# A hybrid decoder layer on one core: recurrence scores in 32-token blocks on quarters of TensorE's array, a query tile in another PSUM bank, and softmax, compression and start-up steps in another order

## The chip, the cores and the metric

The kernel runs on one core of a Trainium2 chip. The metric is the device time of one execution in microseconds (us). A core has five engines that run their own instruction streams side by side: TensorE (PE; its weight loads are listed as PEld), VectorE (DVE), ScalarE (ACT), GpSimd (POOL) and SyncE (SP), which only starts transfers. They meet at semaphores. TensorE multiplies a stationary operand (the weights, up to 128 x 128, loaded first) by a moving one and writes to PSUM, eight banks of 128 partitions x 512 fp32 values. Its 128 x 128 array can be split by columns into two groups of 64 or four of 32, each with weights and an output of its own.

## The reference

One layer on x of shape (1, 1024, 1024), fp32: a feed-forward half step, a token mixer, a second feed-forward half step and a last norm. The mixer's width is shared by an attention of 8 heads of 64 in two key groups (three branches: compressed, selected and window, each with its own softmax and a gate) and a gated linear recurrence of 4 heads of 128.

```python
h = h + 0.5 * swiglu(rms_norm(h, ffn1_norm), ffn1_w_gu, ffn1_w_down)
h = h + hybrid_mixer(rms_norm(h, mix_norm), ...)
h = h + 0.5 * swiglu(rms_norm(h, ffn2_norm), ffn2_w_gu, ffn2_w_down)
return rms_norm(h, final_norm)
# mixer: parts = split(h @ w_in); concat(o_nsa, o_hg) @ w_out

# compressed keys and values of the attention
flat = blocks.transpose(0, 1, 3, 2, 4).reshape(B, nb, G, CMP_LEN * dk)
kc = gelu(flat @ w1) @ w2
# attention, for each of the three branches
p = softmax(where(valid, q @ k.T * scale - slope * dist, NEG)); o = p @ v
o = g[..., 0:1] * o_cmp + g[..., 1:2] * o_sel + g[..., 2:3] * o_win

# recurrence, chunk by chunk of 64 tokens
b = jnp.cumsum(lf, axis=2)                        # lf = log of the forget gate
decay = jnp.exp(where(tril, b[:, :, :, None, :] - b[:, :, None, :, :], NEG))
a = jnp.einsum('bhtd,bhtsd,bhsd->bhts', qc, decay, kc)
o = a @ vc + (qc * jnp.exp(b)) @ state
state = jnp.exp(b_last) * state + (kc * jnp.exp(b_last - b)).T @ vc
```

The decayed scores `a` can be had as plain products: two tokens that fall into different halves of a block of 2m tokens have their decay split at the middle of the block, one factor on the query, one on the key.

## The kernel before

**Dense work.** Every fp32 product of the layer's large matrices is three fast matmuls of 128 x 128 x 512 (high and low parts of both operands, `mm3`, L162 to L164; the same with 256 columns at L769 to L771 and for the down projections at L704 to L706). The splits into parts are made by GpSimd or ScalarE (high, L154 and L156) and VectorE (low, L158). Other work is laid between these matmuls: generators yield after a small piece, and the loops in `body` step them in turn. The order in which the code emits instructions is the order on each engine.

**Scores of the recurrence** (`hgrn_unit`, from L853). A unit is one head and one half of the sequence, 512 tokens in four groups `c` of 128; the two halves of a head are stepped together, so there are four pairs of units. Keys `k` and queries `q` lie as 128 channels x 512 tokens. For the base and for each of seven levels (block size 2m, m = 1 to 64), `score` multiplies keys by queries into a PSUM bank of tag "b", VectorE scales the second half of each block of q and the first half of each block of k by the decay (L893, L894), and the scores of that level are copied under a mask into `B` (L897). Base and levels 0 to 5 compute eight products of 64 x 64 (two per group of 128 tokens, on column groups 0 and 64 of the array, `mm64`); level 6, the off-diagonal 64 x 64 block of each 128, four. Each step yields, and the dense projection that the loop at L1520 walks through runs between two steps. `A` holds the finished score matrix of 128 x 128 per group.

**Compression** (`compress`, L1025 and L1048) is the first thing that this loop steps (hh = 0), with the projection of head 0 as the dense work; its weight tiles `w1` are loaded by ScalarE's queue into four buffers as they come free. What is left of the dense work runs after the steps.

**Query tiles** (`att_proj_q`). Each of four tiles of a half is a bank of 128 x 512; after its 24 dense matmuls ScalarE copies (L1100) and VectorE subtracts (L1101), twice, and the bank is free. At L1544 tiles 0 and 1 of the first half both use tag "b". The next stage's projection starts in tag "b" as well.

**Softmax** (`att_soft`). For each key group and block of 128 queries, four heads hh = 0 to 3 are taken one after the other. Scores of the three branches are reduced by VectorE (L1191), `rest()` takes the exponential on ScalarE with its row sums (L1228); after every second head VectorE inverts the sums of both heads in one instruction (L1232) and GpSimd scales the rows of both, three instructions a head (L1238). `att_pv` then transposes the scaled rows of all four heads on TensorE (L1269).

**Start and the norm chain.** At the start eight slices of x are split (L399, L400), and from kt = 5 the first products' copies out of PSUM (`pp`, L576) stand between them. In the first down projection, a table `after` hooks steps of the next norm (`first`, `cols`) behind certain tiles.

Of the kernel before, what the change touches and what calls it, by code (L numbers as in the profile page):

```python
# [9 lines left out]
F32 = mybir.dt.float32  # L10
F32R = mybir.dt.float32r
I32 = mybir.dt.int32
U8 = mybir.dt.uint8
# [58 lines left out]
class Net:  # L72
# [709 lines left out]
    def mixer_consts(self, tp):  # L782
# [11 lines left out]

        self.id64 = c.tile([128, 64], F32, name="id64")
        for o in (0, 64):
            r, k = slice(o, o + 64), slice(o, o + 64)
            nc.vector.tensor_copy(out=self.id64[r], in_=self.ident[r, k])
            nc.vector.tensor_copy(out=up[r, 64:], in_=xf[r, k])
        xf, up = up[:, 64:], up[:, :64]  # L800
        self.lev = []
        for l in range(5):
            m = 1 << l
            nc.vector.tensor_scalar(up, xf, float(m), None, op0=OP.is_ge)
            k = c.tile([128, 64], U8, name=f"lev{l}")
            nc.vector.scalar_tensor_tensor(out=k[:], in0=xf, scalar=float(2 * m), in1=up,
                                           op0=OP.is_lt, op1=OP.mult)
            self.lev.append(k)
# [45 lines left out]
    def hgrn_unit(self, p, t, half, states, mo):  # L854
# [8 lines left out]

        def mm64(out, part, a, b):
            mm(out[part * 64:part * 64 + 64], k[:, a:a + 64], q[:, b:b + 64], start=True, stop=True,  # L865
               tile_position=(0, part * 64), skip_group_check=True)

        def score(last=False):
            b = self.bank("b")
            for c in range(4):  # L870
                o = c * 128
                if last:
                    mm64(b[:, c // 2 * 64:c // 2 * 64 + 64], c % 2, o, o + 64)
                else:
# [8 lines left out]
        nc.vector.tensor_tensor(out=B[:], in0=b, in1=self.id64[:, None, :].to_broadcast([128, 4, 64]), op=OP.mult)  # L883
        yield
        F, o = f[:], 0
        for l in range(7):
            m = 1 << l
            n = 512 // (2 * m)
            b = score(l == 6)
            F2 = F.rearrange("p (n two) -> p n two", two=2)  # L890
            qv = q[:].rearrange("p (n two m) -> p n two m", two=2, m=m)[:, :, 1, :]
            kv = k[:].rearrange("p (n two m) -> p n two m", two=2, m=m)[:, :, 0, :]
            nc.vector.tensor_tensor(out=qv, in0=qv, in1=F2[:, :, 0:1].to_broadcast([128, n, m]), op=OP.mult)  # L893
            nc.vector.tensor_tensor(out=kv, in0=kv, in1=F2[:, :, 1:2].to_broadcast([128, n, m]), op=OP.mult)  # L894
            nc.vector.tensor_tensor(out=ft[:, o:o + n], in0=F2[:, :, 0], in1=F2[:, :, 1], op=OP.mult)
            if l < 5:
                nc.vector.copy_predicated(out=B[:], mask=self.lev[l][:, None, :].to_broadcast([128, 4, 64]), data=b)  # L897
            elif l == 5:
                for i in (0, 64):
                    nc.scalar.activation(out=B[i:i + 32, :, 32:64], in_=b[i:i + 32, :, 32:64], func=AF.Copy)  # L900
                for i in (0, 64):
                    nc.scalar.activation(out=A[i:i + 64, :, i:i + 64], in_=B[i:i + 64], func=AF.Copy)
            else:
                for i in range(2):
                    nc.scalar.activation(out=A[0:64, i::2, 64:128], in_=b[i * 64:i * 64 + 64, 0:2, :], func=AF.Copy)
            F = ft[:, o:o + n]
            o += n
            yield
# [252 lines left out]
    def att_soft(self, p, g, qb, hh):  # L1161
# [147 lines left out]
def body(ctx, tc, ins, out):  # L1309
# [37 lines left out]
    with cs:  # L1347
# [138 lines left out]

    after[6, 2] = first
    for m, n in zip(range(6, 11), (1, 2, 1, 2, 2)):
# [10 lines left out]
    if True:  # L1499
# [9 lines left out]
        with cw:  # L1509
            with ExitStack() as ch:  # L1510
# [257 lines left out]
```

## Time and profile before

| | us |
|---|---|
| three runs | 2004.4, 2007.15, 2007.25 (median 2007.15) |
| the profiled execution | 2007.51 |
| its span (first to last instruction) | 2005.8 |
| TensorE busy | 1976.2 (99%) |
| VectorE busy | 1390.7 (69%) |
| ScalarE busy | 793.1 (40%) |
| GpSimd busy | 501.7 (25%) |

The span is what the hardware profiler recorded between the first and the last instruction; 1.7 us of the execution lie outside it. Busy time counts an engine's own instructions, and for TensorE the ends of its pipelined matmuls are modelled. The chain that ended last is found by going back from the last instruction, at each step to what released it. The granted clock is 1.00 for TensorE at 2.4 GHz and 0.50 at 1.2 GHz; over the whole execution its mean is 0.997.

### The profile page before, as it was taken

To read this page: it belongs to the slowest core of one execution; us is meant where nothing else is said; L and a number is where in the kernel's file an instruction comes from. 1 tells how busy PE (TensorE), PEld (TensorE's weight loads), DVE (VectorE), ACT (ScalarE), POOL (GpSimd) and SP (SyncE) were. 2 spreads that over 40 slices of the span, in tenths; PEclk is the share of its full clock that TensorE was granted. 3 is DMA by queue.
4 is the path that set the end of the run, shared out by engine and by line. 5 is a ranking of instruction groups with operands and counts; after the bars stand their busy time and mean duration, and the time that the engine had idled before them with its cause. 6 is when DMAs were issued, how large, how long until landed. Compare 5 with 4: busy or idle time off the path is not lost.

```text
span 2005.8 us, 30977 instructions
## 1 busy us (share of the span) xinstructions
PE 1976.2 (99%) x10862; PEld 1661.2 (83%) x10862; DVE 1390.7 (69%) x2843; ACT 793.1 (40%) x1673; POOL 501.7 (25%) x594
## 2 busy tenths in 40 slices
PE   9999999999999999999999999999999999999998
PEld 6888888888888889889877788898888888888886
DVE  5987778658766546766358887746766677558677
ACT  5533333322233323332368776645333333323233
POOL 2133233234331000100035534301112222123221
PEclk9999999999999999999999999999999999999999
DMA  5345666348662233332211022452446566157564
GB/s 190 118 133 196 216 213 227 105 161 282 221 226 103 98 106 116 138 119 106 90 64 38 17 67 77 148 210 95 148 169 213 200 218 212 59 178 254 195 206 139
DMA packets 157116, 304.30 MB, mean 152 GB/s; under 512 B 17536, under 2 KB 39072, under 8 KB 156960
## 3 DMA queue, kind: packets, MB, share of 16 engines
q1 hardware_dynamic: 146896, 285.78, 41.9%
q10 hardware_dynamic: 10064, 16.53, 2.3%
q8 instruction: 86, 1.41, 0.3%
q14 instruction: 70, 0.57, 0.1%
HBM read 213.65 MB, written 88.60 MB: 151 GB/s over the span
## 4 chain that ended last, share of the span: by engine, by line
PE 93%; DVE 3%; ACT 1%; POOL 1%; issue 1%; DMA 1%; SPq 0%; DVEq 0%; ACTq 0%; POOLq 0%
PE b L162 17%; PE b L163 16%; PE b L164 16%; PE b L706 7%; PE b L704 7%; PE b L705 7%; PE b L769 3%; PE b L771 3%; PE b L770 3%; PE b L1269 3%; PE b L1260 3%; PE b L865 2%; PE b L1185 1%; PE b L1186 1%; POOL P L1238 1%
## 5 line engine op out<-in xcount | busy, mean ns | idle before, releaser
L163 PE MATMUL b<-xT,wp 128*128 128x512 f32 x1196 | 466.8, 390 | 1.1 <-DVE xT L400 1.0
L162 PE MATMUL b<-xT,wp 128*128 128x512 f32 x1196 | 466.9, 391 | 0.7 <-ACT xT L399 0.7
L164 PE MATMUL b<-xT,wp 128*128 128x512 f32 x1196 | 465.9, 390 | 0.0
L158 DVE TENSOR_TENSOR dw<-dr,dw 128x512 fp32r<-128x512 f32 x308 | 234.5, 809 | 74.3 <-ACT dw L156 61.5
L162 PEld LDWEIGHTS b<-xT,wp 128*128 128x128 f32 x1196 | 224.9, 188 | 50.1 <-issue 2.0
L163 PEld LDWEIGHTS b<-xT,wp 128*128 128x128 f32 x1196 | 224.9, 188 | 48.8 <-DVE xT L400 2.7
L164 PEld LDWEIGHTS b<-xT,wp 128*128 128x128 f32 x1196 | 224.9, 188 | 46.9
L704 PE MATMUL b<-dw,dw 128*128 128x512 f32 x616 | 240.5, 390 | 1.1 <-DVE dw L158 1.1
L706 PE MATMUL b<-dw,dw 128*128 128x512 f32 x616 | 240.1, 390 | 0.2 <-DVE dw L158 0.2
L705 PE MATMUL b<-dw,dw 128*128 128x512 f32 x616 | 240.0, 390 | 0.0
L156 ACT ACTIVATE wp<-ws 128x512 fp32r<-128x512 f32 x148 | 93.3, 632 | 252.8 <-PE b L163 239.0
L154 POOL TENSOR_SCALAR dw<-dr 128x512 fp32r<-128x512 f32 x154 | 123.2, 806 | 275.0 <-PE b L706 158.6
L156 ACT ACTIVATE dw<-dr 128x512 fp32r<-128x512 f32 x154 | 92.4, 628 | 205.7 <-PE b L704 98.0
L1238 POOL TENSOR_SCALAR P<-P,sm,gate 128x64 f32<-128x64 f32 (+8 forms) x192 | 125.1, 669 | 176.3 <-DVE sm L1232 120.5
L158 DVE TENSOR_TENSOR wp<-ws,wp 128x512 fp32r<-128x512 f32 x148 | 111.3, 754 | 40.4 <-ACT wp L156 40.2
L704 PEld LDWEIGHTS b<-dw,dw 128*128 128x128 f32 x616 | 115.7, 188 | 25.5 <-issue 1.8
L706 PEld LDWEIGHTS b<-dw,dw 128*128 128x128 f32 x616 | 115.7, 188 | 25.0 <-DVE dw L158 1.1
L705 PEld LDWEIGHTS b<-dw,dw 128*128 128x128 f32 x616 | 115.7, 188 | 23.8
L156 ACT ACTIVATE wp<-wr 128x512 fp32r<-128x512 f32 x115 | 72.2, 629 | 155.1 <-PE b L163 131.7
L1228 ACT ACTIVATE P<-P,sm 128x64 f32<-128x64 f32 (+8 forms) x192 | 114.8, 600 | 34.2 <-DVE sm L1191 32.7
L496 POOL TENSOR_TENSOR ws<-wr 128x512 f32<-128x512 f32 x37 | 49.6, 1341 | 297.9 <-DVE wp L158 246.9
L1272 DVE TENSOR_TENSOR pt<-b,ph 128x512 fp32r<-128x512 f32 x148 | 99.3, 689 | 30.1 <-ACT ph L1271 29.3
(302 smaller groups left out, 3879.9 us busy)
## 6 DMA issues: line engine op xcount, KB each, us to landing
dr<-hs SPq DMA_DIRECT2D x242, 256.0 KB, 3.8
wr<-in_ffn_w_gu_dram SPq DMA_DIRECT2D x82, 512.0 KB, 3.9
hs<-hk SPq DMA_DIRECT2D x140, 256.0 KB, 3.7
hs<-wd SPq DMA_DIRECT2D x88, 256.0 KB, 3.1
wd<-in_ffn_w_down_dram SPq DMA_DIRECT2D x84, 256.0 KB, 3.3
dr<-in_ffn_w_down_dram SPq DMA_DIRECT2D x62, 256.0 KB, 4.2
wq<-wo SPq DMA_DIRECT2D x40, 256.0 KB, 3.0
wr<-in_w_in_dram SPq DMA_DIRECT2D x16, 512.0 KB, 4.3
```

What stands on the lines that cost most here:

```text
L154: nc.gpsimd.tensor_scalar(out=hi, in0=src, scalar1=1.0, scalar2=1.0, op0=OP.mult, op1=OP.mult)
L156: nc.scalar.activation(out=hi, in_=src, func=AF.Copy)
L158: eng.tensor_tensor(out=lo, in0=src, in1=hi.bitcast(F32), op=OP.subtract)
L162: mm(ps, wh, xh, start=first, stop=False, skip_group_check=skip)
L163: mm(ps, wh, xl, start=False, stop=False, skip_group_check=skip)
L164: mm(ps, wl, xh, start=False, stop=last, skip_group_check=skip)
L704: mm(bs[t][:], hl[:, c], dh, start=first, stop=False, skip_group_check=True)
L705: mm(bs[t][:], hh[:, c], dh, start=False, stop=False, skip_group_check=True)
L706: mm(bs[t][:], hh[:, c], dl, start=False, stop=last, skip_group_check=True)
L1228: nc.scalar.activation(out=rng[br], in_=rng[br], func=AF.Exp, scale=-1.0, bias=m, accum_out=st[:, 6 + br:7 + br])
L1238: nc.gpsimd.tensor_scalar(out=rng[br], in0=rng[br], scalar1=st[:, 6 + br:7 + br], scalar2=self.gate[:, qb, h * 3 + br:h * 3 + br + 1], op0 ...
L1272: nc.vector.tensor_tensor(out=l[:w], in0=b[:w], in1=h[:w].bitcast(F32), op=OP.subtract)
```

## The change

Five things.

1. `score(l)`: base and levels 0 to 4 compute sixteen products of 32 x 32 on column groups 0, 32, 64 and 96; level 5 computes eight of 32 x 32 between the halves of each 64 tokens, on column groups 0 and 64; level 6 stays. The banks, masks and `B` are 128 wide per unit instead of 256. Level 5 is copied by six ScalarE instructions instead of four, and `A` has two more small fills on GpSimd.
2. Tile 1 of the first two query tiles uses a bank of tag "a" (`"ba"[m]`).
3. In the first round (hh = 0, compression) every third step is followed by no dense step.
4. In `rest()`, heads 0 and 1 are still inverted together after head 1; heads 2 and 3 are each inverted and scaled on their own.
5. At the start the first `next(plain)` comes at kt = 6 instead of 5; the hook `first` moves from after[6, 2] to after[6, 3].

```diff
-        def mm64(out, part, a, b):
-            mm(out[part * 64:part * 64 + 64], k[:, a:a + 64], q[:, b:b + 64], start=True, stop=True,
-               tile_position=(0, part * 64), skip_group_check=True)
-
-        def score(last=False):
-            b = self.bank("b")
+        def score(l):
+            b, m = self.bank("b"), max(32, 1 << l)
+            w = m * 2 if l > 5 else m * 4
             for c in range(4):
-                o = c * 128
-                if last:
-                    mm64(b[:, c // 2 * 64:c // 2 * 64 + 64], c % 2, o, o + 64)
-                else:
-                    for i in range(2):
-                        mm64(b[:, c * 64:c * 64 + 64], i, o + i * 64, o + i * 64)
-            return b[:, :256].rearrange("p (c t) -> p c t", c=4)
+                for i in range(0, 128, 2 * m) if l > 4 else range(0, 128, 32):
+                    o = c % 2 * 64 if l > 5 else i
+                    n = c // 2 if l > 5 else c
+                    a = c * 128 + i
+                    mm(b[o:o + m, n * m:n * m + m], k[:, a:a + m], q[:, a + (l > 4) * m:a + (l > 4) * m + m], start=True,
+                       stop=True, tile_position=(0, o), skip_group_check=True)
+            return b[:, :w].rearrange("p (c t) -> p c t", t=m)
 
         nc.gpsimd.memset(A[64:128, :, 0:64], 0.0)
-        B = p.tile([128, 4, 64], F32, name=self.nm("B"), tag="B", bufs=2)
-        b = score()
+        for i in (32, 96):
+            nc.gpsimd.memset(A[i:i + 32, :, i - 32:i], 0.0)
+        B = p.tile([128, 2, 128], F32, name=self.nm("B"), tag="B", bufs=2)[:, 0].rearrange("p (c t) -> p c t", c=4)
+        b = score(0)
...
-            b = score(l == 6)
+            b = score(l)
...
-                nc.vector.copy_predicated(out=B[:], mask=self.lev[l][:, None, :].to_broadcast([128, 4, 64]), data=b)
+                nc.vector.copy_predicated(out=B, mask=self.lev[l][:, None, :].to_broadcast([128, 4, 32]), data=b)
             elif l == 5:
+                for i in range(0, 128, 32):
+                    nc.scalar.activation(out=A[i:i + 32, :, i:i + 32], in_=B[i:i + 32], func=AF.Copy)
                 for i in (0, 64):
-                    nc.scalar.activation(out=B[i:i + 32, :, 32:64], in_=b[i:i + 32, :, 32:64], func=AF.Copy)
-                for i in (0, 64):
-                    nc.scalar.activation(out=A[i:i + 64, :, i:i + 64], in_=B[i:i + 64], func=AF.Copy)
+                    nc.scalar.activation(out=A[i:i + 32, :, i + 32:i + 64], in_=b[i:i + 32], func=AF.Copy)
...
-            b = self.bank(tag)
+            b = self.bank(tag if tag != "ba" else "ba"[m])
...
-            if hh % 2 == 0:
-                return
-            nc.vector.reciprocal(out=both[:, :, 6:9], in_=both[:, :, 6:9])
-            scaled(h - 1, both[:, 0, :], *before)
-            scaled(h, st, rng)
+            if hh == 1:
+                nc.vector.reciprocal(out=both[:, :, 6:9], in_=both[:, :, 6:9])
+                scaled(h - 1, both[:, 0, :], *before)
+            elif hh:
+                nc.vector.reciprocal(out=st[:, 6:9], in_=st[:, 6:9])
+            if hh:
+                scaled(h, st, rng)
...
-                if kt == 5:
+                if kt == 6:
                     next(plain)
...
-    after[6, 2] = first
+    after[6, 3] = first
...
-                    for _ in steps:
-                        next(dense, None)
+                    for i, _ in enumerate(steps):
+                        if hh or i % 3 < 2:
+                            next(dense, None)
...
-            dense = net.att_proj_q(qp, wq.get, X, 0, "b", (0, 1))
+            dense = net.att_proj_q(qp, wq.get, X, 0, "ba", (0, 1))
```

Names in the instruction orders below: `b` is a PSUM bank's tile, `xT` the split activations, `wh` and `wl` the two parts of a weight tile.

A step of the scores on TensorE before, in the recurrence of head 0 with the dense work of head 1 behind it:

```order
L865 MATMUL b_6790<-q_6217,k_6251 64x64 x8
L865 MATMUL b_6803<-q_6300,k_6341 64x64 x8
L162 MATMUL b_6819<-xT_5674,wh_6725 128x512
L163 MATMUL b_6819<-xT_5675,wh_6725 128x512
L164 MATMUL b_6819<-xT_5674,wl_6726 128x512
```

The same after:

```order
L872 MATMUL b_6830<-q_6221,k_6257 32x32 x16
L872 MATMUL b_6851<-q_6316,k_6366 32x32 x16
L162 MATMUL b_6875<-xT_5702,wh_6749 128x512
L163 MATMUL b_6875<-xT_5703,wh_6749 128x512
L164 MATMUL b_6875<-xT_5702,wl_6750 128x512
```

Twice as many products of a quarter of the outputs stand in front of the same dense matmuls.

TensorE before, at the end of head 0's projection (L771), the compression's steps (L1025; `w` are its weights, `fl` its blocks) and the start of head 1's projection:

```order
L771 MATMUL b_6616<-wh_6347,xT_5689 128x256
L1025 MATMUL b_6606<-fl_6427,w_1301_6492 128x126
L1025 MATMUL b_6607<-fl_6427,w_1301_6492 128x126
L1025 MATMUL b_6606<-fl_6427,w_1301_6492 128x126
L1025 MATMUL b_6607<-fl_6427,w_1301_6492 128x126
L1025 MATMUL b_6606<-fl_6427,w_1305_6529 128x126
L1025 MATMUL b_6607<-fl_6427,w_1305_6529 128x126
L1025 MATMUL b_6606<-fl_6427,w_1305_6529 128x126
L1025 MATMUL b_6607<-fl_6427,w_1305_6529 128x126
L1025 MATMUL b_6606<-fl_6427,w_1313_6608 128x126
L1025 MATMUL b_6607<-fl_6427,w_1313_6608 128x126
```

Twenty-eight products of the compression, in two pieces of twelve and sixteen with four dense matmuls between them, follow the last L771. After:

```order
L771 MATMUL b_6655<-wh_6372,xT_5717 128x256
L1024 MATMUL b_6496<-fl_6504,w_1317_6613 128x126
L1024 MATMUL b_6497<-fl_6504,w_1317_6613 128x126
L1024 MATMUL b_6496<-fl_6504,w_1317_6613 128x126
L1024 MATMUL b_6497<-fl_6504,w_1317_6613 128x126
L162 MATMUL b_6759<-xT_5702,wh_6749 128x512
L163 MATMUL b_6759<-xT_5703,wh_6749 128x512
L164 MATMUL b_6759<-xT_5702,wl_6750 128x512
L162 MATMUL b_6759<-xT_5702,wh_6749 128x512
```

One step of four products (eight passes) is left between the last L771 and head 1's first L162; the others have moved between L771s.

VectorE in the softmax before, from one pair's reciprocal to the next (`sm` the row sums, `P` the rows, ISA the reductions at L1191):

```order
L1232 RECIPROCAL sm_10363<-sm_10363 128x2x3
L1191 ISA P_1835_10446,sm_10447<-b_10448,dwin 128x384
L1191 ISA sm_10447 128x1
L1191 ISA P_10445,sm_10447<-b_10452,dsel 128x384
L1191 ISA sm_10447 128x1
L1191 ISA P_1835_10446,sm_10447<-b_10452,dcmp 128x64
L1191 ISA sm_10447 128x1
```

After, the part with a reciprocal of one head:

```order
L1190 ISA P_1863_10982,sm_10940<-b_10983,dwin 128x384
L1190 ISA sm_10940 128x1
L1233 RECIPROCAL sm_10940<-sm_10940 128x3
L1190 ISA P_10938,sm_10940<-b_10987,dsel 128x384
L1190 ISA sm_10940 128x1
L1190 ISA P_1863_10982,sm_10940<-b_10987,dcmp 128x64
L1190 ISA sm_10940 128x1
```

The reciprocal of head 2's three sums now stands inside head 3's reductions.

## Rows read from the trace of the kernel before

**Rows 1.** The page: span, TensorE's busy time, and the chain by engine.

```profile
span 2005.8 us, 30977 instructions
...
PE 1976.2 (99%) x10862; PEld 1661.2 (83%) x10862; DVE 1390.7 (69%) x2843; ACT 793.1 (40%) x1673; POOL 501.7 (25%) x594
...
PE 93%; DVE 3%; ACT 1%; POOL 1%; issue 1%; DMA 1%; SPq 0%; DVEq 0%; ACTq 0%; POOLq 0%
```

**Rows 2.** TensorE's waits: waiting line, awaited; total us, times, longest.

```profile
PE b L1269 <- POOL P L1238: 4.9, 6, 1.3
...
PE b L704 <- DVE dw L158: 1.1, 2, 0.6
```

**Rows 3.** Groups by shape, TensorE: shape, count | busy us, mean ns of one.

```profile
L865 PE MATMUL b<-q,k 128*64 128x64 f32 x960 | 35.3, 225 | 0.0
...
L209 PE MATMUL b<-sq,o 128*32 128x512 f32 x32 | 5.2, 601 | 0.0
```

**Rows 4.** The chain that ended last, by time: start us, us, what, count.

```profile
21.92 1.85 PE b L209 x16
...
804.66 1.08 PE b L865 x32
...
832.85 0.61 PE b L865 x16
```

**Rows 5.** Two short windows, L209 on TensorE alone: us, busy (records), clock.

```profile
21.80:21.85 0.05, 0.00 (x0) 1.00 1.73 696
21.85:21.88 0.03, 0.03 (x4) 1.00 0.69 273
```

**Rows 6.** Windows: us, busy PE, PEld, DVE, ACT, POOL; clock, DMA.

```profile
804.00:833.00 29.00, 29.00 (x320) 23.01 (x320) 21.42 (x49) 7.13 (x17) 2.49 (x2) 1.00 0.41 146
1004.00:1007.30 3.30, 2.93 (x7) 2.39 (x8) 0.57 (x3) 1.33 (x3) 0.00 (x0) 0.50 0.00 0
741.10:744.40 3.30, 3.30 (x12) 2.82 (x11) 0.00 (x0) 2.49 (x4) 0.00 (x0) 0.50 0.60 203
1085.00:1100.00 15.00, 13.50 (x76) 10.56 (x75) 12.50 (x35) 14.52 (x38) 7.94 (x13) 1.00 0.16 55
```

**Rows 7.** Groups by shape, VectorE: masked copies and reciprocals.

```profile
L897 DVE COPY_PREDICATED B<-lev,b 128x256 f32<-128x256 uint8 x40 | 17.6, 441 | 0.0
...
L1232 DVE RECIPROCAL sm<-sm 128x6 f32<-128x6 f32 x32 | 6.0, 188 | 7.3 <-ACT P L1228 6.9
```

**Rows 8.** TensorE's timeline: start, us, what [idle before <- releaser].

```profile
13.66 0.47 PE L162 MATMUL b<-xT,wp 128*128 128x512 f32 x1 [0.71 <-ACT xT L399]
14.35 0.50 PE L163 MATMUL b<-xT,wp 128*128 128x512 f32 x1 [0.22 <-DVE xT L400]
...
731.54 2.84 PE L1025 MATMUL b<-fl,w 128*128 128x126 f32 x24
...
740.56 1.67 PE L1025 MATMUL b<-fl,w 128*128 128x126 f32 x8 [2.06 <-DMA w<-in_cmp_v_w_dram]
...
1004.37 0.77 PE L162 MATMUL b<-xT,wh 128*128 128x512 f32 x1 [2.37 <-issue]
...
1007.40 0.39 PE L163 MATMUL b<-xT,wh 128*128 128x512 f32 x1
1007.63 0.40 PE L164 MATMUL b<-xT,wl 128*128 128x512 f32 x1
```

**Rows 9.** Timelines of ScalarE and VectorE at the second query copy.

```profile
1002.95 0.59 ACT L1100 ACTIVATE qa<-b 64x512 fp32r<-64x512 f32 x1 [0.75 <-DVE qa L1101]
...
1003.57 0.69 DVE L1101 SCALAR_TENSOR_TENSOR qa<-b,qa 64x512 fp32r<-64x512 f32 x1 [0.66 <-ACT qa L1100]
```

**Rows 10.** Timelines of GpSimd and VectorE at head 1's weight split.

```profile
731.79 2.05 POOL L154 TENSOR_SCALAR wh<-wr 128x1024 fp32r<-128x1024 f32 x2 [27.98 <-PE b L771]
...
732.87 3.18 DVE L158 TENSOR_TENSOR wl<-wr,wh 128x1024 fp32r<-128x1024 f32 x2 [0.53 <-POOL wh L154]
```

**Rows 11.** GpSimd's timeline: six scalings of two heads.

```profile
1064.62 3.33 POOL L1238 TENSOR_SCALAR P<-P,sm,gate 128x384 f32<-128x384 f32 x6 [0.63 <-DVE sm L1232]
```

More of the change, by code (lines that the diff above doesn't have):

```diff
@@ L793, in mixer_consts @@
         nc.vector.tensor_tensor(out=xf, in0=xf, in1=up, op=OP.mult)
[L795 to L800, printed above, removed]
+        self.id32 = c.tile([128, 64], F32, name="id32")[:, :32]
+        for o in range(0, 128, 32):
+            r = slice(o, o + 32)
+            nc.vector.tensor_copy(out=self.id32[r], in_=self.ident[r, r])
+            nc.vector.tensor_copy(out=up[r, 96:], in_=xf[r, r])
+        xf, up = up[:, 96:], up[:, :32]
         self.lev = []
@@ L804, in mixer_consts @@
             nc.vector.tensor_scalar(up, xf, float(m), None, op0=OP.is_ge)
-            k = c.tile([128, 64], U8, name=f"lev{l}")
-            nc.vector.scalar_tensor_tensor(out=k[:], in0=xf, scalar=float(2 * m), in1=up,
+            k = c.tile([128, 64], U8, name=f"lev{l}")[:, :32]
+            nc.vector.scalar_tensor_tensor(out=k, in0=xf, scalar=float(2 * m), in1=up,
                                            op0=OP.is_lt, op1=OP.mult)
@@ L860, in hgrn_unit @@
         ft = p.tile([128, 512], F32, name=self.nm("ft"), tag="ft", bufs=2)
-        def mm64(out, part, a, b):
-            mm(out[part * 64:part * 64 + 64], k[:, a:a + 64], q[:, b:b + 64], start=True, stop=True,
-               tile_position=(0, part * 64), skip_group_check=True)
-        def score(last=False):
-            b = self.bank("b")
-            for c in range(4):
-                o = c * 128
-                if last:
-                    mm64(b[:, c // 2 * 64:c // 2 * 64 + 64], c % 2, o, o + 64)
-                else:
-                    for i in range(2):
-                        mm64(b[:, c * 64:c * 64 + 64], i, o + i * 64, o + i * 64)
-            return b[:, :256].rearrange("p (c t) -> p c t", c=4)
+        def score(l):
+            b, m = self.bank("b"), max(32, 1 << l)
+            w = m * 2 if l > 5 else m * 4
+            for c in range(4):
+                for i in range(0, 128, 2 * m) if l > 4 else range(0, 128, 32):
[5 more added lines that the diff above has]
+            return b[:, :w].rearrange("p (c t) -> p c t", t=m)
         nc.gpsimd.memset(A[64:128, :, 0:64], 0.0)
-        B = p.tile([128, 4, 64], F32, name=self.nm("B"), tag="B", bufs=2)
-        b = score()
+        for i in (32, 96):
+            nc.gpsimd.memset(A[i:i + 32, :, i - 32:i], 0.0)
+        B = p.tile([128, 2, 128], F32, name=self.nm("B"), tag="B", bufs=2)[:, 0].rearrange("p (c t) -> p c t", c=4)
+        b = score(0)
         nc.vector.tensor_tensor(out=q[:], in0=q[:], in1=f[:], op=OP.mult)
-        nc.vector.tensor_tensor(out=B[:], in0=b, in1=self.id64[:, None, :].to_broadcast([128, 4, 64]), op=OP.mult)
+        nc.vector.tensor_tensor(out=B, in0=b, in1=self.id32[:, None, :].to_broadcast([128, 4, 32]), op=OP.mult)
         yield
@@ L896, in hgrn_unit @@
             if l < 5:
-                nc.vector.copy_predicated(out=B[:], mask=self.lev[l][:, None, :].to_broadcast([128, 4, 64]), data=b)
+                nc.vector.copy_predicated(out=B, mask=self.lev[l][:, None, :].to_broadcast([128, 4, 32]), data=b)
             elif l == 5:
+                for i in range(0, 128, 32):
+                    nc.scalar.activation(out=A[i:i + 32, :, i:i + 32], in_=B[i:i + 32], func=AF.Copy)
                 for i in (0, 64):
-                    nc.scalar.activation(out=B[i:i + 32, :, 32:64], in_=b[i:i + 32, :, 32:64], func=AF.Copy)
-                for i in (0, 64):
-                    nc.scalar.activation(out=A[i:i + 64, :, i:i + 64], in_=B[i:i + 64], func=AF.Copy)
+                    nc.scalar.activation(out=A[i:i + 32, :, i + 32:i + 64], in_=b[i:i + 32], func=AF.Copy)
             else:
                 for i in range(2):
-                    nc.scalar.activation(out=A[0:64, i::2, 64:128], in_=b[i * 64:i * 64 + 64, 0:2, :], func=AF.Copy)
+                    nc.scalar.activation(out=A[0:64, i::2, 64:128], in_=b[i * 64:i * 64 + 64], func=AF.Copy)
             F = ft[:, o:o + n]
```

## The prediction

> **What bounds the kernel now.** I read the page first. TensorE is busy for 1976.2 of a span of 2005.8 us, and the chain that ended last runs on it for 93% [rows 1]. So an edit is worth what it takes from TensorE's own time or from its waits; work on the other engines counts only where TensorE waits for it. The table of waits comes next: the longest entry is 4.9 us in 6 waits for the softmax scalings on GpSimd [rows 2]; the longest single waits, 2.37 and 2.06 us, stand in the timeline [rows 8]. Span less busy time is 29.6 us, 1.5%: all that waits can give. A change can therefore win either such waits or the matmuls themselves; the largest part here does the second. The profiled execution took 2007.51 us (1.7 us outside its span); the sum is made against it, and the median of the three runs, 2007.15 us, is 0.4 us less.
>
> **Scores, the largest part.** L865 issues 960 passes (each fp32 matmul shows as two), mean 225 ns [rows 3]. They come in steps: the same level of two units, 32 passes, for 1.08 us of the chain; the last level has 16 passes and 0.61 us [rows 4]. So 16 passes cost 0.47 us, 29.4 ns a pass with two 64-column groups of the array side by side, and 0.14 us per step is the way in and out. There are four pairs of units with seven steps of 32 passes: 28 steps. The change makes 24 of them (base and levels 0 to 4) 64 passes of 32x32, four groups abreast, and 4 of them (level 5) 32 passes of 32x32, two abreast. The sixteen-pass step stays.
>
> Lower bound: if groups run truly side by side, a half as wide pass takes half the time and twice as many run at once, so 64 passes take 64 x 7.35 ns = 0.47 us, the step 0.61 us, and 0.47 us is saved in each of 28 steps: -13.2 us. Upper bound: no L865 row shows passes fed faster than one per 29.4 ns; at that rate a step takes 64 x 29.4 ns + 0.14 = 2.02 us, 0.94 us more in 24 steps, +22.6 us (level 5 keeps its count and its time). The row nearest to the new form is L209's: 128x32 weights in four column groups. Its 32 passes last 601 ns on average, 19.2 us in all, in 5.2 us of busy time, 3.7 abreast [rows 3]; four of them begin inside 0.03 us, after none in the 0.05 us before [rows 5]; 16 take 1.85 us of the chain [rows 4]. So four groups do run together, and a start costs under 10 ns. What that row doesn't show is 64 short passes in one stream: its fours are 0.4 us apart, which gives time to refill. I take three quarters of the gain, **-10 us**, and keep both ends.
>
> What hides the rest: VectorE takes each score from PSUM. Between 804 and 833 us, seven steps with the dense work between them, it is busy 21.42 of 29 us [rows 6]. Seven steps shorter by 0.36 us leave 26.5 us, still over its 21.4. Its copies of 441 ns [rows 7] have half the elements, so they shorten, which I count at nothing (0 to -0.2 us each, off the path). The two small GpSimd fills per unit and the two more ScalarE copies at level 5 are beside that work too: ScalarE is busy 7.13 and GpSimd 2.49 of the 29 us [rows 6].
>
> **Query tile in another bank.** TensorE stands still for 2.37 us ahead of the L162 at 1004.37 [rows 8]. It wants the bank in which tile 1 lies, and that bank is being emptied by ScalarE and VectorE in turn: the second pair of copies runs from 1002.95 to 1004.26 [rows 9]. After the stop the granted clock is 0.50 for the window 1004.0 to 1007.3 [rows 6], 1.2 instead of 2.4 GHz, with TensorE idle just before; half of 3.3 us is lost, 1.65 us. With tile 1 in bank "a" the first dense tile of the next stage waits for nothing of this. What is late next is the tile that follows in bank "a": twelve dense matmuls stand ahead of it, at the 0.23 us between two starts [rows 8] about 2.7 us, and the copies end 2.3 us after TensorE's stop. That covers them by 0.4 us. **-4.0 us**, bounds 0 and -4.0.
>
> **Compression steps.** Every third step of the first round now issues no dense step, so dense work is left for the end. Before, the last steps run back to back, and TensorE waits 2.06 us for a weight's transfer at 740.56 [rows 8]; the granted clock is then 0.50 from 741.1 to 744.4 [rows 6], 1.65 us lost. Together -3.7 us. But what lies ahead of head 1's first projection gets shorter: its weight split on GpSimd starts at 731.79, released by the last L771, and VectorE's halves follow from 732.87 at 1.59 us each [rows 10]. The first low half is ready at 734.46, 2.67 us after the release. Now only eight compression passes, at 2.84 us for 24 [rows 8], and two dense ones (0.95 + 0.46 us) stand ahead of the L164 that needs it: a new wait of 1.3 us. **-2.4 us**; bounds -3.7 (split in time) and +1.3 (the weight still late, and the new wait).
>
> **Reciprocals and row scalings.** Six scalings in a row follow head 3's reciprocal, 3.33 us [rows 11], 0.56 us each, and the transposes wait for them six times, at most 1.3 us [rows 2]. With head 2's three scaled earlier, head 3's come 1.7 us sooner, more than any of the six waits. Lower bound -4.9 us [rows 2]. Upper bound: 16 more reciprocals at 188 ns [rows 7], all on the path, +3.0 us. VectorE and ScalarE are nearly full there: from 1085 to 1100 ScalarE works 14.52 of 15 us [rows 6], so a wait that leaves GpSimd can come back as one for ScalarE. I take half: **-2.5 us**.
>
> **Start, and the norm chain.** One ScalarE xT goes ahead of the two pp copies. TensorE waits there 0.71 and 0.22 us [rows 8]: **-0.9 us**, bounds 0 and -0.9. The "first" hook one step later moves a chain of VectorE behind a pair of weight splits; L704 waits 1.1 us in 2 waits for splits in the whole run [rows 2]. Taken at nothing, bounds -1.1 and +1.1.
>
> **The sum.** -10 - 4.0 - 2.4 - 2.5 - 0.9 = -19.8 us: 1987.7 us against the profiled execution, 1987.4 against the median. I say **1987 us**, about 1% faster. All lower bounds together are -27.8 us, 1979 us.
>
> **Rivals.**
> *The passes are fed too slowly* (slower). If TensorE can be handed a new pass only every 29.4 ns, the scores cost +22.6 us, and with the other parts (-9.8) the time is +12.8, 2020 us. It becomes slower than before from 22 ns a pass: then each of 24 steps costs 0.49 us more, 11.7 us, which is all that the other parts (9.8) and level 5 (1.9) give. For it: no stretch of L865 is faster, and the records double for the same arithmetic. Against it: the four starts inside 0.03 us [rows 5]. The Trainium skill, "TensorE: Matmul & The Clock Gate", section "Wait — 56ns, not 53.3ns?", says that starts never come closer than about 25 ns however small the matmul; by that figure the estimate would be 2012 us, and the four starts inside 0.03 us don't agree with it for four column groups, while no row here shows a longer stream of them.
> *The feed is half as fast as needed.* At 14.7 ns a pass 64 passes take 0.94 us: the 24 steps stay at 1.08 us, only level 5's 1.9 us and the 9.8 us of the rest come: 1995.4 us. For it: the stream of 64 that no row shows.
> *The waits come back.* The scores give their 10 us, but the softmax stage waits for ScalarE instead, and the projection's split and the bank's next tile take back most of the rest; 2 us of 9.8 stay: 1995 us.
> *The scores don't set the end* where VectorE, not TensorE, is late, and the rest comes to nothing: within 4 us of 2007.
>
> **How the numbers follow.** Forecast 0.60 (1979 to 1992), half feed 0.17 (1992 to 2003), waits come back 0.10 (1992 to 2000), no change 0.04, slow feed 0.09 (2011 to 2020 and over). Leaving out the last two and the tails, the range is 1979 to 2002. A measurement of this kernel tells apart about 0.2%, 4 us. Faster 0.87, same 0.04, slower 0.09.
>
> **What would show it.** Steps of the scores with 64 passes should read about 0.7 us in the chain, 0.61 at best, and over 1.08 where the feed is slow. The wait at about 1004 and both stretches at a granted clock of 0.50 should be gone; a wait at the L164 or L162 ahead of head 1's projection should be there, about 1.3 us; the table of waits should show under 2.5 us for POOL's scalings. If score steps read 1 us or more, the largest term is wrong; if they read 0.7 and the time is still above 1995, waits have taken the rest.

## The result and the profile after

The changed kernel takes 1983.99 us (median of four runs, 1983.4 to 1985.38) against 2007.2 us for the kernel before on the same chip: a ratio of 0.9887, 95% interval 0.987 to 0.9904, 23 us faster. Measured again on another chip it was 0.9896 (0.9881 to 0.9911). The prediction said 1987 us, range 1979 to 2002. The profiled execution took 1985.38 us, 1.7 us of it outside the span; it is 22.1 us shorter than the profiled one before, for which the sum had said 19.8.

The page after, the lines that answer to [rows 1]: span, busy time, and the chain by engine.

```profile
span 1983.7 us, 32563 instructions
...
PE 1960.7 (99%) x11630; PEld 1647.2 (83%) x11630; DVE 1388.0 (70%) x2863; ACT 795.1 (40%) x1689; POOL 508.1 (26%) x610
...
PE 88%; DVE 4%; issue 3%; ACT 2%; DMA 1%; POOL 1%; SPq 0%; ACTq 0%; DVEq 0%; POOLq 0%
```

TensorE's count of matmuls rises by 768, as the diff says, and its busy time falls by 15.5 us. It still bounds the kernel.

TensorE's waits after: who waits for whom, total us, times, longest.

```profile
PE b L1261 <- ACT ph L1272: 2.2, 4, 0.7
PE b L162 <- DVE pd L660: 1.6, 1, 1.6
PE b L704 <- DVE dw L158: 1.3, 2, 0.7
...
PE b L872 <- DVE q L881: 0.8, 2, 0.5
```

Three waits that the prediction priced are gone: the six for GpSimd [rows 2], the one at L162 and the one for the compression weight [rows 8]. The waits of L704 for splits are still there. The wait for pd is new. It is not the change's: seven kernels that leave out one or more of its parts show it at 0.2 to 1.5 us, whether the start was changed or not, and only the one profile of before shows none. It hangs on when a weight's transfer lands: GpSimd's split of that weight waits for it until 343.74 us in the trace of before and until 344.67 in this one.

Both stretches at half clock [rows 6] are gone too; only the last 5.3 us of the span have a granted clock of 0.50. Two windows, at the start of head 1's projection and behind the query tile (us, busy PE, PEld, DVE, ACT, POOL; clock, DMA):

```profile
739.00:742.00 3.00, 3.00 (x32) 2.32 (x34) 1.53 (x3) 2.65 (x5) 2.68 (x5) 1.00 0.28 87
989.00:992.00 3.00, 3.00 (x16) 2.49 (x16) 1.68 (x4) 2.23 (x3) 0.00 (x0) 1.00 0.00 0
```

To see where the time went, take the same dense matmul in both traces (the sequence of the dense matmuls is the same) and compare the time between two of them. Bounds are in us of the kernel before; the matmuls taken start there at 1.25, 19.95, 689.97, 748.95, 957.02, 1001.72, 1007.86, 1142.13 and 1990.05.

```
from to (before)   before    after    change  forecast
   1 to   20        18.70    17.87    -0.8     -0.9   start
  20 to  690       670.02   672.41    +2.4      0     feed-forward 1, norm
 690 to  749        58.98    54.93    -4.0     -2.4   compression, and two score steps (-0.8)
 749 to  957       208.07   197.82   -10.3    -10     the other score steps
 957 to 1003        44.70    44.70     0        0
1003 to 1008         6.14     2.22    -3.9     -4.0   query tile
1008 to 1142       134.27   129.09    -5.2     -2.5   softmax
1142 to 1990       847.92   847.67    -0.2      0
```

Of the +2.4 us, 1.6 lie between 340 and 400 us, at the pd wait, and 0.6 between 400 and 520. In the traces of the experiments the first stretch takes 60.1 to 61.4 us whatever the kernel; before's 59.9 is the shortest of all. The start varies as well: 16.9 to 18.5 us in the nine traces with the new start, 18.5 to 19.6 in the five with the old one.

The group of the new passes (TensorE, by shape: count | busy us, mean ns of one), to set beside [rows 3]:

```profile
L872 PE MATMUL b<-q,k 128*32 128x32 f32 x1664 | 21.5, 199 | 1.1 <-DVE q L881 0.8 <-DVE k L893 0.3
```

A pass of half the width still lasts 199 ns instead of 225, so its length says little; how close the starts lie tells what a step costs.

### The profile page after: what moved, and what is told of

Read it like the earlier page. It is cut to its first block, busy times and chain, and to the rows that moved or that the text cites. A ratio compares the mean times of both kernels' runs of the same rounds, so it can differ in the third digit from the quotient of the medians.

```text
span 1983.7 us, 32563 instructions
## 1 busy us (share of the span) xinstructions
PE 1960.7 (99%) x11630; PEld 1647.2 (83%) x11630; DVE 1388.0 (70%) x2863; ACT 795.1 (40%) x1689; POOL 508.1 (26%) x610
## 4 chain that ended last, share of the span: by engine, by line
PE 88%; DVE 4%; issue 3%; ACT 2%; DMA 1%; POOL 1%; SPq 0%; ACTq 0%; DVEq 0%; POOLq 0%
PE b L162 16%; PE b L163 16%; PE b L164 16%; PE b L706 6%; PE b L704 6%; PE b L705 6%; PE b L769 3%; PE b L770 3%; PE b L771 3%; PE b L1261 3%; PE b L1270 3%; PE b L1185 1%; PE b L1184 1%; PE b L872 1%; ACT P L1227 1%
## 5 line engine op out<-in xcount | busy, mean ns | idle before, releaser
L162 PE MATMUL b<-xT,wp 128*128 128x512 f32 x1196 | 466.3, 390 | 1.9 <-DVE pd L660 1.6
L164 PE MATMUL b<-xT,wp 128*128 128x512 f32 x1196 | 465.3, 389 | 0.0
L162 PEld LDWEIGHTS b<-xT,wp 128*128 128x128 f32 x1196 | 224.6, 188 | 51.7 <-issue 2.0
L164 PEld LDWEIGHTS b<-xT,wp 128*128 128x128 f32 x1196 | 224.5, 188 | 46.9
L704 PE MATMUL b<-dw,dw 128*128 128x512 f32 x616 | 240.2, 390 | 1.3 <-DVE dw L158 1.3
L704 PEld LDWEIGHTS b<-dw,dw 128*128 128x128 f32 x616 | 115.6, 188 | 25.7 <-issue 2.1
```

Of the source, the lines that this page charges most:

```text
L162: mm(ps, wh, xh, start=first, stop=False, skip_group_check=skip)
L164: mm(ps, wl, xh, start=False, stop=last, skip_group_check=skip)
L704: mm(bs[t][:], hl[:, c], dh, start=first, stop=False, skip_group_check=True)
```

## Experiments

### The scores alone, and all but the scores

The edit of the first is part 1 of the diff with nothing else; of the second, parts 2 to 5 with `score` as before.

> The kernel before with the first part alone (scores in 32x32 blocks on four column groups). Theory A (the array bounds a step, four groups abreast): each of the 24 steps of 64 passes takes some 0.40 us less from one dense matmul to the next, each of the 4 of level 5 too, 28 x 0.40 = 11.2 us, so about 1996 us; the waits at L162 of 2.4 us and for the compression weight of 2.1 us stay. Theory B (TensorE is made faster, but VectorE then sets the pace of the recurrence and the other parts were needed for the gain): under 6 us of gain, with new waits of TensorE for VectorE between the steps.

> The changed kernel with the scores as before (64x64 blocks on two column groups); everything else changed. Theory A (the parts add up): 22 to 23 us less 11.2 us, so 11 to 12 us faster than before, about 1995.5 us. Theory B (a shorter recurrence lets the waits of the later stages fall, the gains belong together): less than 8 us faster, over 1999 us.

The scores alone give 0.9948 (0.9933 to 0.9963), 1995.35 against 2005.17 us; the rest alone 0.994 (0.9926 to 0.9955), 1994.43 us. That is 10 and 12 us, and together they make the ratio 0.9888: the parts add up, theory A twice. TensorE's timeline of the scores alone (start, us, what) shows one step and the dense matmul behind it.

```profile
756.32 0.76 PE L872 MATMUL b<-q,k 128*32 128x32 f32 x64
757.01 0.51 PE L162 MATMUL b<-xT,wh 128*128 128x512 f32 x1
```

From the step's first pass to the next dense matmul 0.69 us pass, against 1.08 in [rows 4]. That is 0.39 us in each of 24 steps; the four of level 5 take 0.63 us, 0.45 less. Together it is 11 us.

### Why a step is short: the order on the column groups

The next kernel issues the same sixteen products of a unit's step, group by group instead of in turn:

```diff
-            for c in range(4):
-                for i in range(0, 128, 2 * m) if l > 4 else range(0, 128, 32):
+            for c, i in ([(c, i) for i in range(0, 128, 32) for c in range(4)] if l < 5 else
+                         [(c, i) for c in range(4) for i in range(0, 128, 2 * m)]):
```

> The changed kernel with the same products of base and levels 0 to 4 in another order: four products in a row on column group 0, then four on group 32, 64, 96, instead of one on each in turn. Theory A (the gain is that neighbours in the stream run on different column groups): eight passes in a row share a group and follow each other at 27 to 30 ns, a step takes 1.8 us instead of 0.57, 24 steps, about 30 us over the changed kernel, 2014 us. Theory B (the queue in front of the array finds work for the other groups by itself, and the gain is only that a product is smaller): within 3 us of the changed kernel, 1984 us.

2001.3 us in one run, 17 us over the changed kernel; between the marks 749 and 957 the trace has 16 us more. TensorE's timeline, one step and the dense matmul that follows:

```profile
755.97 1.51 PE L872 MATMUL b<-q,k 128*32 128x32 f32 x64
...
757.41 0.50 PE L162 MATMUL b<-xT,wh 128*128 128x512 f32 x1
```

With a pass of 0.20 us (the group above) the first and the last start lie 1.31 us apart, 21 ns a pass; in turn it is 0.76 - 0.20 = 0.56 us, 9 ns a pass. So it is the neighbours in the stream that must lie on different groups, theory A; the size was too high (30 us). In the trace nearly all gaps between starts are 25 to 32 ns or 5 to 6 ns, so the runs of two groups overlap in part. Smaller products in a bad order would have been slower than the kernel before: 1.44 us a step against 1.08.

### How fast passes can be fed

Base and levels 0 to 4 go over the sixteen products twice, so a step is 128 passes; the values stay what they were.

```diff
-            for c in range(4):
+            for c in [*range(4), *range(4)] if l < 5 else range(4):
```

> The changed kernel, but base and levels 0 to 4 issue each round of sixteen 32x32 products a second time into the same place, so that a step has 128 passes in one stream (the values stay the same). It measures how fast TensorE can be fed in a long stream. Theory A (the array bounds it, four abreast at 7.9 ns a pass as in the first passes of a step now): the added 64 passes take 0.51 us a step, 24 steps, 12 us over the changed kernel, about 1996 us. Theory B (the first passes of a step come from a queue that was filled ahead, the rest is fed at the rate of the rival in the prediction, 14.7 ns or more): 0.94 us or more a step, 23 us or more, over 2007 us.

2005.62 us in one run, 21.6 us over the changed kernel; between the marks 749 and 957 the trace has 20.2 us more, 22 steps. Three steps of TensorE's timeline, and a later wait:

```profile
870.70 1.46 PE L872 MATMUL b<-q,k 128*32 128x32 f32 x128
875.03 1.46 PE L872 MATMUL b<-q,k 128*32 128x32 f32 x128
879.39 1.36 PE L872 MATMUL b<-q,k 128*32 128x32 f32 x128
...
887.62 0.50 PE L164 MATMUL b<-xT,wl 128*128 128x512 f32 x1 [1.84 <-issue]
```

TensorE's waits in the same run:

```profile
PE b L872 <- issue: 2.3, 3, 1.1
...
PE b L164 <- issue: 1.8, 1, 1.8
...
PE b L770 <- issue: 0.9, 1, 0.9
```

In the 21 steps without a stop the first and the last start lie 1.13 to 1.33 us apart, median 1.17. That is 0.6 us more than in a step of 64, or 9.4 ns for each added pass: a little over theory A's 7.9. The rest are stops. TensorE stands still five times, 5.0 us in all and 4.0 of them between the marks, and waits for nothing that the table of waits shows. Behind the longest stop the granted clock is 0.50 for 3.4 us, which costs 1.7 us:

```profile
888.20:891.60 3.40, 3.40 (x9) 2.32 (x7) 0.00 (x0) 0.00 (x0) 0.00 (x0) 0.50 0.41 158
```

With all of it an added pass costs 20.2 / (22 x 64) = 14.3 ns; less the stops and the half clock it is 10.3. So it is chance that 14.3 lies at the half feed that the prediction held as a rival (14.7 ns): in no step without a stop do the starts lie more than 10.5 ns apart on average. The changed kernel has no such stop.

What the stops are can be read from the trace, though no run was made for it. Two DMA queues carry transfers that the profile calls "instruction". One has 70 of them in either kernel; here is the other's line on the page of the changed kernel, then on the page of this one (transfers, MB, share):

```profile
q8 instruction: 92, 1.51, 0.3%
```

```profile
q8 instruction: 104, 1.70, 0.4%
```

Twelve more transfers come with 1536 more matmuls (13166 against 11630) and as many weight loads, so one transfer brings 256 of them. Counted through the whole run, all five stops lie at the same place in such a group of 256, behind 193 or 194 of it, and each ends 1.3 to 1.6 us after a transfer on that queue has landed. By this TensorE had run out of instructions: a step of 128 passes, with its weight loads, is 256 by itself. Theory A is right on the pace; the sum is neither theory's.

### The softmax part alone, and a reciprocal for every head

The first is part 4 of the diff by itself. The second goes on from the changed kernel:

```diff
-            if hh == 1:
-                nc.vector.reciprocal(out=both[:, :, 6:9], in_=both[:, :, 6:9])
-                scaled(h - 1, both[:, 0, :], *before)
-            elif hh:
-                nc.vector.reciprocal(out=st[:, 6:9], in_=st[:, 6:9])
-            if hh:
-                scaled(h, st, rng)
+            nc.vector.reciprocal(out=st[:, 6:9], in_=st[:, 6:9])
+            scaled(h, st, rng)
```

> The kernel before with only the reciprocals and row scalings of heads 2 and 3 taken one by one. Theory A (all of what the softmax stage gained comes from this part): the TensorE time of the stage from 1005 us to the end of the attention falls by 5 us and the six waits of 4.9 us for GpSimd are gone; about 2002 us. Theory B (my prediction: ScalarE and VectorE take half back, the rest of the gain came from elsewhere, for instance a stage that begins with the full clock): 2 to 3 us, about 2004.5 us, with waits for ScalarE in place of those for GpSimd.

> The changed kernel with the reciprocals and row scalings of heads 0 and 1 taken one by one too, so that no head shares. Theory A (the softmax stage gained because the last heads' scalings no longer stand behind those of the head before): heads 0 and 1 are early anyway, nothing to gain, within 1.5 us of the changed kernel. Theory B (the gain was a more even load on GpSimd and VectorE): 1 to 3 us more. Theory C (VectorE is the bound there, 16 more reciprocals of 0.19 us on the path): up to 3 us slower.

Alone the part gives 0.9978 (0.9967 to 0.9989), 2001.7 us, and its stretch from 1008 to 1142 falls from 134.27 to 130.14 us, 4.1 of the 5.2. Here is the table of TensorE's waits in that stage, all that is left:

```profile
PE b L162 <- issue: 2.4, 1, 2.4
PE b L1262 <- DVE pt L1274: 1.2, 2, 0.9
PE b L1185 <- DVE sm L1191: 1.0, 4, 0.5
PE b L1262 <- ACT ph L1273: 0.9, 2, 0.5
PE b L1186 <- DVE kl L1159: 0.4, 1, 0.4
```

The kernel before had, beside its six waits for GpSimd, these two lines in the same stretch:

```profile
PE b L1260 <- ACT ph L1271: 1.2, 4, 0.4
...
PE b L1260 <- DVE pt L1272: 0.3, 1, 0.3
```

No wait for GpSimd is left, those for ScalarE are 0.9 us instead of 1.2, and those for VectorE's `pt` rose from 0.3 to 1.2: theory A, with a little given back on VectorE. That part, a wait of 0.9 us for `pt`, is most of what lies between 4.1 and 5.2 us: the trace of the full change doesn't have it, the one with level 5 on four groups (below) does. A reciprocal for every head changes nothing that can be told: 1984.23 us beside 1985.33 for the changed kernel on the same chip, 129.46 us in the stage against 129.01. Only the last heads stood in the way.

The gain can exceed the 4.9 us that I had as the lower bound, because the table's idle time begins at the modelled end of the matmul before. Two waits of the kernel before:

```profile
1045.56 0.48 PE L163 MATMUL b<-xT,wh 128*128 128x512 f32 x1
1046.81 0.44 PE L1269 MATMUL b<-ident,P 128*128 128x128 f32 x2 [0.76 <-POOL P L1238]
```

The matmul at 1045.56 is shown to end at 1046.04, but a dense matmul is followed by the next 0.23 us after its start [rows 8]. Without the wait the transposes would have begun near 1045.8: the wait cost 1.0 us, not 0.76. If the other five are like it, six waits with 0.25 us more each make 6.4 us; that is an estimate from this one.

### Compression: alone, and left out

The first is part 3 alone, the second all of the change but part 3.

> The kernel before with only the compression steps spread. Theory A: the wait of 2.1 us for the weight and the stretch at half clock after it go, 3.7 us, less new waits of TensorE for VectorE at the first score steps of some 0.4 us: 3.3 us faster, about 2004 us. Theory B (my prediction): the weights of head 1's projection come late, a new wait of 1.3 us at an L164, 2.4 us faster. Theory C: the transfer is only late elsewhere, no gain.

> The changed kernel with the compression steps as before (a dense step after every one of them). Alone, this part took 3.6 us out of its stretch of the trace, but only 1 us (3.0 faster to 0.8 slower) out of the times. Theory A (the trace is right, the time alone was too coarse): the wait for the compression weight, 1.6 to 3.7 us in five traces, and in most of them a stretch at a granted clock of 0.50 come back at about 735 us; 3 us slower than the changed kernel, ratio to the kernel before about 0.9905. Theory B (what the part gives there is lost again further on, for instance in the transfers of the feed-forward part behind it): the wait comes back, and the time stays within 1 us of the changed kernel, ratio about 0.989.

The trace of the first shows the 3.6 us (58.98 to 55.41 in its stretch), and TensorE's timeline shows no late weights at head 1's projection:

```profile
737.88 1.05 PE L1025 MATMUL b<-fl,w 128*128 128x126 f32 x8
738.70 0.47 PE L162 MATMUL b<-xT,wh 128*128 128x512 f32 x1
739.01 0.39 PE L163 MATMUL b<-xT,wh 128*128 128x512 f32 x1
739.24 0.39 PE L164 MATMUL b<-xT,wl 128*128 128x512 f32 x1
...
744.01 0.69 PE L865 MATMUL b<-q,k 128*64 128x64 f32 x16 [0.57 <-DVE q L882]
744.94 0.69 PE L865 MATMUL b<-q,k 128*64 128x64 f32 x16 [0.24 <-DVE q L882]
```

The L164 for which I had forecast 1.3 us doesn't wait; two score steps wait 0.8 us for VectorE instead. My theory B falls. The weight's split on GpSimd that I had read as head 1's is the one after it; head 1's stands 30 us earlier in the kernel before:

```profile
701.56 2.26 POOL L154 TENSOR_SCALAR wh<-wr 128x1024 fp32r<-128x1024 f32 x2 [21.72 <-PE b L163]
731.79 2.05 POOL L154 TENSOR_SCALAR wh<-wr 128x1024 fp32r<-128x1024 f32 x2 [27.98 <-PE b L771]
```

But the times don't show the 3.6 us. Alone: 2004.43 against 2005.17 us, 0.9995 (0.9985 to 1.0004). Left out: 1985.1 us, 0.9884 (0.9868 to 0.9901), no slower than the changed kernel's 0.9887 and 0.9896. In that last trace the wait came back with 0.9 us in two parts, and the stretch is 0.8 us longer than in the changed kernel:

```profile
738.72 1.16 PE L1024 MATMUL b<-fl,w 128*128 128x126 f32 x8 [0.60 <-DMA w<-in_cmp_v_w_dram]
...
740.16 1.16 PE L1024 MATMUL b<-fl,w 128*128 128x126 f32 x8 [0.28 <-DMA w<-in_cmp_v_w_dram]
```

So the cost of this wait is not a property of the kernel alone. In the six traces without part 3 it was 0.9, 1.6, 2.0, 2.1, 2.5 and 3.7 us, and the half clock followed it in those with 2.0, 2.1, 2.5 and 3.7 us, not in the other two.

How often it followed can be read from the mean granted clock of every run. No trace with a stretch at half clock ahead of its end shows a mean above 0.998. Of the 19 runs of the kernel before that stand beside part 3 alone, 10 have 0.999 (median 2004.5 us), 5 have 0.998 (2006.4) and 4 have 0.997 (2007.8). The profiled execution has 0.997 and both stretches [rows 6]; the median run, 2005.17 us at 0.999, had neither by this measure. Compared at the same clock, part 3 alone is 1.1 to 1.2 us faster (four runs at 0.999, five at 0.998), near the 0.8 us in the traces with and without it above. That is an estimate from few runs; by the interval the part is worth between nothing and 3 us, which stays open.

### The query tile and the start

The second and fifth parts of the diff, each alone.

> The kernel before with only query tile 1 in a bank of tag a. Theory A (wait and half clock are one loss and go together): the wait of 2.4 us at L162 is gone, no stretch at a granted clock of 0.50 near 1004 us, TensorE's time between the last score step and the softmax stage falls by 4 us. Theory B: the wait moves to the twelve dense matmuls' successor, the first tile in bank a, and 1 to 2 us of it stay.

> The kernel before with only the start (kt = 6) and the hook of the norm chain (after[6, 3]) changed. Theory A: 0.7 to 0.9 us less before 15 us, the two waits for xT there gone; the waits of L704 for splits near 631 us as before; less than 1 us in all, which one run cannot tell from no change. Theory B: the earlier start makes the weights of the first feed-forward part come late, and the wait of L162 for pd near 348 us (1.6 us in the changed kernel, none in the kernel before) comes from this part: then it is there, and it is absent where the start is as before.

With the bank changed, the wait at L162 is gone and the stretch from 1003 to 1008 falls from 6.14 to 2.22 us, theory A, the same 3.9 us as in the full change. The time, 2004.74 beside 2005.86 us in one run each, doesn't show it, and the reason stands in the trace: the granted clock fell in the softmax stage instead, twice. Two windows (us, busy PE, PEld, DVE, ACT, POOL; clock, DMA):

```profile
1112.00:1114.00 2.00, 2.00 (x11) 1.82 (x10) 1.55 (x6) 0.70 (x3) 1.53 (x2) 0.50 0.03 8
1128.00:1131.00 3.00, 3.00 (x14) 2.62 (x12) 2.19 (x8) 2.55 (x7) 1.27 (x3) 0.51 0.00 0
```

Ahead of the first, TensorE had idled three times in 3 us:

```profile
1107.88 0.66 PE L1269 MATMUL b<-ident,P 128*128 128x128 f32 x4 [0.57 <-POOL P L1238]
1108.95 0.49 PE L1260 MATMUL b<-ph,vhl 128*128 128x512 f32 x1 [0.28 <-ACT ph L1271]
1110.10 0.50 PE L1185 MATMUL b<-ka,qa 128*128 128x512 f32 x1 [0.65 <-DVE sm L1191]
```

The stage took 136.70 us, 2.4 more than before. The same waits, 0.57, 0.27 and 0.64 us, stand in the kernel before, where the clock stayed at 1.00 in this stage.

The start alone took 0.8 us off its own stretch (18.70 to 17.86) and showed the pd wait at 0.5 us, less than the 1.4 and 1.5 us in two kernels with the old start, so that theory B falls. Its time, 2009.97 us in one run, is 4 us above the kernel before; TensorE happened to wait 3.7 us for the compression weight there, with 6.8 us at half clock behind it:

```profile
PE b L1025 <- DMA w<-in_cmp_v_w_dram: 3.7, 1, 3.7
```

### Level 5 on four groups

If neighbours on more groups are what counts, the four steps of level 5, which use two groups, have something left. The changed kernel, beside itself on the same chip:

```diff
-            w = m * 2 if l > 5 else m * 4
+            w = m * 2 if l > 4 else m * 4
...
-                    o = c % 2 * 64 if l > 5 else i
-                    n = c // 2 if l > 5 else c
+                    o = c % 2 * 64 if l > 5 else i + c % 2 * 32 if l == 5 else i
+                    n = c // 2 if l >= 5 else c
...
-                    nc.scalar.activation(out=A[i:i + 32, :, i + 32:i + 64], in_=b[i:i + 32], func=AF.Copy)
+                    for c in range(2):
+                        nc.scalar.activation(out=A[i:i + 32, c::2, i + 32:i + 64], in_=b[i + c * 32:i + c * 32 + 32], func=AF.Copy)
```

> The changed kernel again, on the chip of the next two, as their neighbour. Expected: 0.987 to 0.990 of the kernel before, as in its first measurement, and no stretch at a granted clock of 0.50 before the last 7 us.

> The changed kernel with the eight products of level 5 on all four column groups (every second group of 128 tokens 32 partitions further up) and two more small copies on ScalarE. Theory A (neighbours on more groups run side by side): the four steps of level 5, 0.50 us now for 32 passes, take 0.26 us, 1 us less in all, which the time can hardly show but the trace can. Theory B (the copies of ScalarE come late and the next use of the bank waits): no gain, a new wait of TensorE for ScalarE at these steps.

The changed kernel came out as expected: 0.9896, and no half clock ahead of its last 5.5 us. Its step of level 5, from the trace of its first measurement:

```profile
821.71 0.70 PE L872 MATMUL b<-q,k 128*32 128x32 f32 x32
```

and with four groups:

```profile
819.78 0.46 PE L872 MATMUL b<-q,k 128*32 128x32 f32 x32
```

0.24 us less in each of four steps, and the stretch from 749 to 957 is 197.29 us against 198.47: theory A. In time 1984.12 us beside 1985.33, 0.989 (0.9873 to 0.9906) against 0.9896 (0.9881 to 0.9911), which can't be told apart. It is the better version by the trace alone.

## Why the prediction was right, point by point

**What bounds the kernel.** Right: the gain is 11 us of TensorE's own work and the rest waits and half clock. That the sum comes so near, -22.1 us for -19.8, is in part luck: the softmax gave 2.7 us more than its term and the scores 1 us, and 2.4 us were lost in a stretch that the change doesn't touch.

**Scores.** Forecast -10 us, measured -11 in the trace and -10 alone in time. The two ends and the row that chose between them held: L209 [rows 3 to 5] showed four groups abreast, and a step comes to 0.69 us where 0.61 was the best and "about 0.7" the forecast. The reason for keeping a quarter back, a long stream, held only in part: a pass costs 8.4 ns in a step of 32, 9 in one of 64, and 9.4 when added to that. The rival's 14.7 ns didn't come as a steady feed; at 128 passes TensorE keeps its pace and then stops for instructions. The Trainium skill, "TensorE: Matmul & The Clock Gate", section "Wait — 56ns, not 53.3ns?", has starts never closer than about 25 ns; the 64 passes whose starts lie within 0.56 us don't agree with it where neighbours run on four column groups. With eight passes in a row on one group the mean was 21 ns.

**Query tile.** Forecast -4.0, measured -3.9 us twice. The next tile in bank "a" didn't wait. The half clock behind the wait was taken as its sure consequence, and that is not so: it came in four of the five traces with the wait, but with the softmax part alone the wait was there and the clock stayed at 1.00.

```profile
1005.75 0.47 PE L162 MATMUL b<-xT,wh 128*128 128x512 f32 x1 [2.38 <-issue]
```

```profile
1006.00:1008.00 2.00, 2.00 (x10) 1.64 (x10) 0.00 (x0) 0.72 (x3) 0.00 (x0) 1.00 0.00 0
```

The first is TensorE's timeline there, the second a window behind it with the clock in the third column from the right. The stretch from 1003 to 1008 took 4.78 us in that execution instead of 6.14, so without the half clock the part is worth 2.6 us (down to 2.22), not 4.0.

**Compression.** The -2.4 stands near the -3.2 of the trace only because two errors work against each other. The step that failed is "its weight split on GpSimd starts at 731.79": that split belongs to the tile after head 1's first, and the new wait of 1.3 us never came. In its place the first score steps wait 0.8 us for VectorE, which the prediction didn't have. And the 3.7 us for the wait and the half clock were taken from one execution as if each had them; in time the part is worth 0 to 3 us, about 1 us at the same clock.

**Softmax.** The mechanism was right and the size was off: -2.5 forecast, -5.2 in the full change and -4.1 alone. The term mis-sized is the half that ScalarE was to take back. TensorE's waits for it fell from 1.2 to 0.9 us, although it worked 14.52 of 15 us [rows 6]; the part adds nothing to its work. The lower bound of -4.9 us was too near, because idle time in the table understates what a wait costs.

**Start and norm chain.** -0.8 for -0.9 in the one pair of traces, within a spread of over 1 us between traces with the same start; the hook did nothing that can be told.

## What to carry to other kernels

Smaller products paid here because neighbours in the stream lie on different column groups, and then even twice the number of passes is cheaper: 64 passes in turn took 0.69 us a step where 32 of twice the width took 1.08, and the same 64 in group order 1.44. How long such a stream may be is also a matter of instructions: at 128 passes a step TensorE ran out of them. A wait behind a transfer should be priced from several traces, not one, and a half clock after a wait is a chance, not a cost. When a wait's cause is looked up, follow the number of the tile, not the line: the same line splits every weight.

## What the runs showed of the hardware that was not expected

- Passes of 128x32 weights by 32 columns, fp32, in turn on four column groups start every 9 ns (64 in 0.56 us) and on two groups every 16 ns (32 in 0.50 us); with 32 on four groups it is 8.4 ns (0.26 us).
- With 128 such passes in a step the starts keep to 9 to 10.5 ns, but TensorE stood still five times, for 0.16 to 1.84 us. All five stops lie at the same place in a group of 256 matmuls and weight loads, which is what one transfer on the instruction queue brings.
- The granted clock fell to 0.50 for some 3 us after waits, and whether it did differed between executions: after 2.37 us of idling it fell (before), after 2.38 us it didn't (softmax part alone), and after 0.57, 0.28 and 0.65 us within 3 us it did (bank alone), where the kernel before idled as long and it didn't. Of 19 runs of the kernel before on one chip, 10 show a mean of 0.999, and no trace with such a stretch ahead of its end shows more than 0.998.
